# A mixture-of-experts stage: the side work of an expert unit gathered into one block, biases and embedding loaded a unit earlier

## The chip, the cores and the metric

The kernel runs on one core of a Trainium2 chip. The metric is device time in microseconds (us) of one execution. The engines are TensorE (PE, with its weight loads shown apart as PEld), VectorE (DVE), ScalarE (ACT), GpSimd (POOL) and SyncE (SP), whose queue issues most DMA transfers.

## The reference, cut to what matters

A first layer (attention beside a gated delta net) is followed by a second block on 256 tokens of width 1024: a mixer, a mixture of experts, a gate that adds a projected embedding, and a final norm. The change lies in the mixture of experts and in the place where the embedding is projected.

```python
def moe(u, w_router, b_router, w_gu, b_gu, w_dn, b_dn):      # 32 experts, top 4, 256 tokens
    ...
    def expert_block(args):
        e, xs = args
        hh = jnp.dot(xs, w_gu[e]) + b_gu[e]                  # 1024 -> 2048
        glu, lin = jnp.split(hh, 2, axis=-1)
        glu = jnp.minimum(glu, SWIGLU_LIMIT)
        lin = jnp.clip(lin, -SWIGLU_LIMIT, SWIGLU_LIMIT)
        act = glu * jax.nn.sigmoid(SWIGLU_ALPHA * glu) * (lin + 1.0)
        return jnp.dot(act, w_dn[e]) + b_dn[e]               # 1024 -> 1024
    ...
    yr = yb.reshape(n_rows, d) * row_gate[:, None].astype(yb.dtype)
    y = jax.ops.segment_sum(yr, row_tok, num_segments=t + 1)[:t]

# second_block, behind the mixer
    h = h + moe(rmsnorm_2(h, g_moe[i]), w_router[i], b_router[i], w_gu[i], b_gu[i], w_dn[i], b_dn[i])
    u = rmsnorm_2(h, g_ple[i])
    h = h + jax.nn.sigmoid(u @ w_ple_gate[i]) * (p[i] @ w_ple_proj[i])
```

## The kernel before

The mixture of experts takes about 1000 us of the time, from some 575 to 1572 us of the span. Each expert serves up to 64 tokens in a block. All 32 experts' weights are read: per expert 8 tiles of 1 MiB for the first product (`w_gu`, "gu" below) and 4 for the second (`w_dn`, "dn"), 384 transfers in all, issued by SP (L110) into 15 buffers in rotation, named raw, whi and wlo. `refill` issues the next transfer once a buffer is free and keeps 14 in hand, one fewer for each entry of `held`.

`run` (L1417) goes over 17 units. Unit 0 is one expert; units 1 to 7 and 9 to 16 are pairs, whose two experts' products use 64 columns each on the two halves of the TensorE array; unit 8 is one expert with two blocks of 64 tokens, which uses all 128 columns (L1445). In step i of the loop the gu products of unit i go into four PSUM tiles ph (L1455, 64 of them in a pair), the results are copied to hs (L1500, on DVE and ACT), and then the dn products of unit i - 1 go into two of the four PSUM tiles pm (L1455, 32 in a pair). `gated` (L1392, L1393) scales the result by the gates and `combine` puts the rows back to their tokens (PE L1401, DVE L1404).

Everything else of a unit is side work, written as generators that pause at each `yield`:

- `gather`: four comparisons on DVE (L1316) make the selection dd, 16 products of 128 columns (L1325) pick the tokens' rows, ACT copies them to xs (L1326). It runs for the unit after next.
- `activation`: 16 transposes of hs (L298; L1361 for the single unit), bias additions on DVE (L1372), clamps (L1376, L1378), Silu (ACT), and the product of both halves (L1381), in two halves z.
- `scatter_rows`: the comparisons dg (L1336), two transposes (L298), and their uses (L1343, L1344).
- `biases`: two transposes of the gates, then four products with the dn biases (L1551), once, in unit 3. `embed`: four transposes and eight products (L1623), once, near the end.

Before, a list `chores` holds these generators, and after every few products `chore()` runs one of them up to its next `yield`. The kernel is then built by a framework that keeps its own order of the instructions on each engine, so the order on an engine is not that of the code: rows of the order, where shown below, are the built kernel's. The place that the step of the loop takes for the products is this:

```python
                        for j in (0, 2):
                            products(kd, hp, k, x, ws, 0, 8, (j, j + 1))
                            if j:
                                refill()
                            chore()
```

Of the kernel before, what the change touches and what calls it, by code (L numbers as in the profile page):

```python
# [15 lines left out]
P = 128  # L16
# [50 lines left out]
def tile_net(ctx: ExitStack, tc: tile.TileContext, a: dict, dbg=None):  # L67
# [144 lines left out]
    def drain(g):  # L212
        for _ in g:
            pass
# [870 lines left out]
    with ExitStack() as c3:  # L1085
# [258 lines left out]
            V.tensor_reduce(b["gs"], ps.rearrange("p t k -> p (t k)"), AX.X, ALU.add)  # L1344
            yield

        def activation(b):

            kd = kind(b)
            n = 1 if kd == "single" else 2  # L1350
            m = 8 // n
            for z in range(n):
                gl = []
                for i in range(2):
                    ps = pm.tile([P, m, 64 * n], F32, name="pm")
                    for c_ in range(m):
                        q, k = (z * m + c_) // 2, c_ % 2
                        h = b["hs"][i][:, q * 2 * P + k:(q + 1) * 2 * P:2]
                        if n == 1:

                            T.matmul(ps[:, c_], h, cc("fold"), start=True, stop=True)  # L1361
                        else:
                            transpose(ps[:, c_], h)
                    gl.append(ps)
                for i in range(2):
                    ps = gl[i]
                    g = gl[i] = wk.tile([P, m, 64 * n], F32, name="sw", bufs=4)
                    cs = slice(i * 8 + z * m, i * 8 + z * m + m)
                    if kd == "pair":
                        bi = bguT[:, b["at"]:b["at"] + 2, cs].rearrange("p e c -> p c e")  # L1370
                        bi = bi[:, :, :, None].broadcast_to([P, m, 2, 64])
                        V.tensor_tensor(g.rearrange("p c (e s) -> p c e s", e=2), ps.rearrange("p c (e s) -> p c e s", e=2), bi, ALU.add)  # L1372
                    else:
                        V.tensor_tensor(g, ps, bc(b["places"][0]["bias"]()[:, cs], 64 * n), ALU.add)
                    if i:
                        V.tensor_scalar(g, g, 7.0, -7.0, ALU.min, ALU.max)  # L1376
                    else:
                        V.tensor_scalar(g, g, 7.0, None, ALU.min)  # L1378
                        A.activation(g, g, AF.Silu, scale=1.702)
                g, l = gl  # L1380
                V.scalar_tensor_tensor(g, l, 1.0, g, ALU.add, ALU.mult)  # L1381
                act = wk.tile([P, m, 64 * n], F32, name="act", bufs=4)
                A.activation(act, g, AF.Copy, scale=1 / 1.702)
                b["act"].append(act)
                yield
# [31 lines left out]
        def run(units, order, ready, more=None, room=None):  # L1417
# [36 lines left out]
                            first, last = c_ < 2, c_ >= nchunks - 2  # L1454
                        T.matmul(o[64 * i:64 * i + 64], x(i, c_), w_[:, zz, sl], start=first, stop=last)  # L1455

            chores = []

            def chore():
                while chores:  # L1460
                    try:
                        next(chores[0])
                        return
                    except StopIteration:
                        chores.pop(0)

            def flush():
                while chores:
                    chore()

            def after(i):
                chores.extend(f(held) for f in more.get(i, ()))

            for _ in gather(units[0]):
                pass
            after(-1)
            if n > 1:
                chores.append(gather(units[1]))
            done = []
            for i in range(n + 1):  # L1480
                if i < n:
                    b = units[i]
                    kd = kind(b)
                    xs = b["xs"]
                    x = lambda h, c_: xs[:, c_] if h is None else xs[:, c_, 64 * h:64 * h + 64] if kd == "pair" else xs[:, c_, :64]
                    hp = [ph.tile([P, 512], F32, name="ph") for _ in range(4)]
                    k = 0
                    while k < 8:
                        ws = [nxt() for _ in range(1 if kd == "double" else 2)]
                        for j in (0, 2):  # L1490
                            products(kd, hp, k, x, ws, 0, 8, (j, j + 1))
                            if j:
                                refill()
                            chore()
                        k += 2 if kd == "single" else 1
                    flush()
                    b["act"] = []
                    b["hs"] = [wk.tile([P, D], F32, name="hs", bufs=2) for _ in range(2)]
                    for j in (0, 2, 1, 3):
                        (V.tensor_copy if j // 2 else A.copy)(b["hs"][j // 2][:, j % 2 * 512:j % 2 * 512 + 512], hp[j])  # L1500
                    chores.append(activation(b))
                    if i == n - 1:
                        while len(b["act"]) < (1 if kd == "single" else 2):
                            chore()
                    chores.append(scatter_rows(b))
                if i:
                    b = units[i - 1]
                    kd = kind(b)
# [6 lines left out]
                    for q in range(4):  # L1515
                        ws = [nxt() for _ in b["places"]]
                        for z in range(0, 2, 2 if kd == "single" else 1):
                            products(kd, yp, 2 * q + z, x, ws, z, 8)
                            chore()
                        refill()  # L1520
                        if i == n:
                            chore()
                    while "gs" not in b:
                        chore()
                    gated(b, yp, room)
                    if i == n:
                        done.append(b)
                    else:
                        chores.append(combine(b))
                if i + 2 < n:  # L1530
                    chores.append(gather(units[i + 2]))
                after(i)
            flush()
            return done[0]

        def biases(held):

            gT = wk.tile([P, 2, P], F32, name="gT")
            bdn = [wk.tile([P, 512], F32, name="sw", bufs=4) for _ in range(2)]
            for nh in range(2):  # L1540
                nc.gpsimd.dma_start(bdn[nh][:NE], a["b_dn_2"][0][:, nh * 512:nh * 512 + 512])
            ps = pm.tile([P, 2, P], F32, name="pm")
            for t in range(2):
                transpose(ps[:NE, t], gate[:, t])
# [7 lines left out]
                    V.tensor_tensor(hres[:, t, ns], hres[:, t, ns], ps, ALU.add)  # L1552
                    yield

        nov = []

        def blocks(held):
            nov.append(nc.values_load(novi[0:1, 0:1], min_val=0, max_val=NJ))
# [40 lines left out]


        big = raw2, RAW2
        pv = []

        def embed(held):

            held.append(1)
            w_ = load(a["w_ple_proj_2"][0], 2, D)
            pt = wk.tile([P, 2, 256], F32, name="sw", bufs=4)
            nc.gpsimd.dma_start(pt, a["p_2"][0, 0].rearrange("(t p) d -> p t d", p=P))
            ps = pm.tile([P, 2, 2, P], F32, name="pm")  # L1610
            for t in range(2):
                for k in range(2):
# [13 lines left out]
            held.pop()  # L1626

        first = [lambda held, g=g: g() for g in (chosen, gates, changes, overflow)]
        last = run(units, order, ready, {-1: first, 2: [biases], 4: [blocks], len(units) - 3: [embed]})

        if "h3" in dbg:
            SY.dma_start(dbg["h3"].rearrange("(t p) d -> p t d", p=P), hres)
# [88 lines left out]
```

## Time and profile before

| | us |
|---|---|
| median of 3 runs | 1619.8 (1618.88 to 1620.29) |
| the profiled execution | 1618.85 |
| its span | 1617.1 |
| PE busy | 1550.6 (96%) |
| DVE busy | 630.6 (39%) |
| ACT busy | 420.5 (26%) |
| POOL busy | 27.9 (2%) |

The span is what the profiler sees between the first and the last instruction; the execution's own time is 1.75 us longer. Busy time of PE is counted from the start to the modelled end of its instructions, so that an engine that is busy all the time is not one at its peak. The trace has two records for each fp32 product: "x16" in a row of the trace are 8 products. The order counts products.

### The profile page before, as it was taken

The numbers are of one execution on the slowest core, as the hardware profiler recorded it, in microseconds if no ns is written. First come the engines' busy times: TensorE is split into PE (matmuls) and PEld (weight loads), VectorE is DVE, ScalarE is ACT, GpSimd is POOL, SyncE is SP. The second block draws the span as 40 slices with busy tenths as digits, with TensorE's granted clock in tenths as the row PEclk, the third lists the DMA queues.
The fourth block names the chain that finished last, engine by engine and source line by source line (L and its number), as shares of the span: only waits on it lengthen the run. The fifth ranks groups of instructions, "written<-read, shape, count | busy, mean of one in ns | idle before, by whom it ended". The sixth has DMA issues, their size and how long they took to land.

```text
span 1617.1 us, 20473 instructions
## 1 busy us (share of the span) xinstructions
PE 1550.6 (96%) x8162; PEld 955.7 (59%) x8162; DVE 630.6 (39%) x1183; ACT 420.5 (26%) x648; POOL 27.9 (2%) x39
## 2 busy tenths in 40 slices
PE   6999999999889989999999999999999999999996
PEld 6889899999688765444444444444444444444335
DVE  6867665456656651321321321331132132131136
ACT  4644554344457421110110110111011011011024
POOL 0000000000000000000000000000000000000001
PEclk9999999999899979999999999999999999999998
DMA  6443333345344199999999999999999999999981
GB/s 207 157 156 107 104 105 105 108 155 195 119 154 137 52 391 408 402 411 364 419 405 418 420 417 419 416 348 387 372 421 411 419 421 415 417 420 413 415 330 54
DMA packets 99247, 484.89 MB, mean 300 GB/s; under 512 B 10470, under 2 KB 14060, under 8 KB 49996
## 3 DMA queue, kind: packets, MB, share of 16 engines
q1 hardware_dynamic: 99004, 483.14, 75.8%
q8 instruction: 66, 1.08, 0.3%
q0 software_dynamic: 144, 0.39, 0.1%
q14 instruction: 33, 0.27, 0.0%
HBM read 482.46 MB, written 1.05 MB: 299 GB/s over the span
## 4 chain that ended last, share of the span: by engine, by line
PE 87%; DVE 7%; ACT 3%; issue 2%; POOL 1%; DMA 1%; SPq 0%; POOLq 0%; DVEq 0%; ACTq 0%
PE ph L1455 32%; PE pm L1455 14%; PE pm L298 5%; PE pm L1325 4%; PE pm L205 4%; PE pm L206 4%; PE pm L204 4%; DVE wlo L310 2%; PE pm L1401 2%; PE ph L1445 2%; PE pm L169 1%; PE pm L170 1%; PE pm L168 1%; ACT whi L309 1%; PE pm L626 1%
## 5 line engine op out<-in xcount | busy, mean ns | idle before, releaser
L1455 PE MATMUL ph<-raw,xs 128*64 128x512 f32 x928 | 266.4, 601 | 0.0
L1455 PE MATMUL ph<-whi,xs 128*64 128x512 f32 x528 | 198.5, 605 | 0.0
L1455 PE MATMUL ph<-wlo,xs 128*64 128x512 f32 x528 | 196.0, 599 | 0.0
L310 DVE TENSOR_TENSOR wlo<-raw,whi 128x2048 fp32r<-128x2048 f32 (+4 forms) x73 | 158.1, 2166 | 77.6 <-ACT whi L309 77.4
L204 PE MATMUL pm<-w,whi 128*128 128x256 f32 x640 | 183.1, 287 | 2.9 <-ACT w L309 2.0
L206 PE MATMUL pm<-w,wlo 128*128 128x256 f32 x640 | 179.3, 281 | 2.7 <-DVE wlo L310 2.7
L205 PE MATMUL pm<-w,whi 128*128 128x256 f32 x640 | 179.7, 281 | 1.9 <-DVE w L310 1.9
L1455 PEld LDWEIGHTS ph<-raw,xs 128*64 128x64 f32 x928 | 91.6, 137 | 139.6 <-issue 137.5
L309 ACT CAST whi<-raw 128x2048 fp32r<-128x2048 f32 (+4 forms) x73 | 131.9, 1808 | 153.7 <-PE pm L205 86.4
L1500 DVE COPY hs<-ph 128x512 f32<-128x512 f32 x34 | 23.5, 692 | 346.3 <-PE ph L1455 328.9
L1455 PE MATMUL pm<-raw,act 128*64 128x512 f32 x520 | 155.1, 598 | 0.0
L204 PEld LDWEIGHTS pm<-w,whi 128*128 128x128 f32 x640 | 122.2, 191 | 3.7 <-ACT w L309 2.5
L206 PEld LDWEIGHTS pm<-w,wlo 128*128 128x128 f32 x640 | 122.0, 191 | 3.1 <-DVE wlo L310 3.1
L205 PEld LDWEIGHTS pm<-w,whi 128*128 128x128 f32 x640 | 122.1, 191 | 2.7 <-DVE w L310 2.6
L1500 ACT COPY hs<-ph 128x512 f32<-128x512 f32 x34 | 18.4, 588 | 352.0 <-PE ph L1455 336.0
L1455 PEld LDWEIGHTS ph<-whi,xs 128*64 128x64 f32 x528 | 60.4, 138 | 80.0 <-issue 78.7
L1455 PEld LDWEIGHTS ph<-wlo,xs 128*64 128x64 f32 x528 | 59.4, 136 | 79.8 <-issue 79.0
L1455 PEld LDWEIGHTS pm<-raw,act 128*64 128x64 f32 x520 | 48.1, 136 | 71.7 <-issue 67.4
L1455 PE MATMUL pm<-wlo,act 128*64 128x512 f32 x232 | 90.2, 599 | 0.0
L1455 PE MATMUL pm<-whi,act 128*64 128x512 f32 x240 | 85.6, 598 | 0.0
L1326 ACT COPY xs<-pm 128x512 f32<-128x512 f32 (+1 forms) x34 | 19.5, 573 | 247.5 <-PE pm L1325 247.5
L1325 PEld LDWEIGHTS pm<-dd,w 128*128 128x128 f32 x544 | 66.8, 200 | 26.6 <-issue 25.7
(403 smaller groups left out, 2009.6 us busy)
## 6 DMA issues: line engine op xcount, KB each, us to landing
raw<-in_w_gu_dram SPq DMA_DIRECT2D x116, 1024.0 KB, 10.5
whi<-in_w_gu_dram SPq DMA_DIRECT2D x70, 1024.0 KB, 12.6
wlo<-in_w_gu_dram SPq DMA_DIRECT2D x70, 1024.0 KB, 10.7
raw<-in_w_dn_dram SPq DMA_DIRECT2D x65, 1024.0 KB, 7.6
raw<-in_w_in_dram SPq DMA_DIRECT2D x46, 1024.0 KB, 5.0
whi<-in_w_dn_dram SPq DMA_DIRECT2D x32, 1024.0 KB, 7.5
wlo<-in_w_dn_dram SPq DMA_DIRECT2D x31, 1024.0 KB, 7.6
raw<-in_w_branch_a_dram SPq DMA_DIRECT2D x4, 1024.0 KB
```

Of the source, the lines that this page charges most:

```text
L204: T.matmul(o, hi[:, k, ns], xh[:, k0 + k], start=first, stop=False)
L205: T.matmul(o, hi[:, k, ns], xl[:, k0 + k], start=False, stop=False)
L206: T.matmul(o, lo[:, k, ns], xh[:, k0 + k], start=False, stop=last)
L298: T.transpose(out, in_, ident[:k, :k])
L309: A.copy(hi, src)
L310: (by or V).tensor_tensor(lo, src, hi.bitcast(F32), ALU.subtract)
L1325: T.matmul(ps[:, c_, :n], ut[t][:, ds_], dd[:, t, :nb], start=t == 0, stop=t == 1)
L1326: A.copy(b["xs"][:, 4 * z:4 * z + 4, :n], ps[:, :, :n])
L1401: T.matmul(pss[nh], b["oh"][:, t], y[:, ns], start=i == 0, stop=i == 1)
L1445: T.matmul(o, x(None, chunk), ws[0][:, z, sl], start=chunk == 0, stop=chunk == nchunks - 1)
L1455: T.matmul(o[64 * i:64 * i + 64], x(i, c_), w_[:, zz, sl], start=first, stop=last)
L1500: (V.tensor_copy if j // 2 else A.copy)(b["hs"][j // 2][:, j % 2 * 512:j % 2 * 512 + 512], hp[j])
```

## The change

- The list `chores` and its steps between products go. All side work of a step of the loop is put into a list `todo` and run in one piece by `flush()`, behind the dn products.
- `activation` is split by its halves z into two generators, with `scatter_rows` between them.
- `gather` for the unit after next is started (its comparisons L1316) right behind the copies to hs, and so are the comparisons dg of `scatter_rows`; their products are run by `flush()`.
- `load_biases` loads the dn biases in step 2, `biases` uses them in step 3 (before, both in step 2's list). `load_embed` loads the embedding and its weight one step before `embed` uses them, and reserves a buffer (`held`) from then on. The small loads get tiles of their own, named bdn (before: two of the four tiles sw).
- The order of copies, sizes, engines and the arithmetic stay.

The diff, cut to its core:

```diff
-        def activation(b):
+        def activation(b, z):
...
-            for z in range(n):
+            if z < n:
...
-            chores = []
-
-            def chore():
-                while chores:
-                    try:
-                        next(chores[0])
-                        return
-                    except StopIteration:
-                        chores.pop(0)
+            todo = []
+
+            def start(g):
+
+                next(g, None)
+                todo.append(g)
 
             def flush():
-                while chores:
-                    chore()
+                for g in todo:
+                    drain(g)
+                todo.clear()
...
-                        for j in (0, 2):
-                            products(kd, hp, k, x, ws, 0, 8, (j, j + 1))
-                            if j:
-                                refill()
-                            chore()
+                        products(kd, hp, k, x, ws, 0, 8, range(4))
+                        refill()
                         k += 2 if kd == "single" else 1
-                    flush()
                     b["act"] = []
...
-                    chores.append(activation(b))
-                    if i == n - 1:
-                        while len(b["act"]) < (1 if kd == "single" else 2):
-                            chore()
-                    chores.append(scatter_rows(b))
+                    if i + 2 < n:
+                        start(gather(units[i + 2]))
+                    sc = scatter_rows(b)
+                    next(sc)
+                    todo += [activation(b, 0), sc, activation(b, 1)]
...
                             products(kd, yp, 2 * q + z, x, ws, z, 8)
-                            chore()
                         refill()
-                        if i == n:
-                            chore()
-                    while "gs" not in b:
-                        chore()
                     gated(b, yp, room)
                     if i == n:
                         done.append(b)
                     else:
-                        chores.append(combine(b))
-                if i + 2 < n:
-                    chores.append(gather(units[i + 2]))
+                        todo.append(combine(b))
+                flush()
                 after(i)
...
-        def biases(held):
-
-            gT = wk.tile([P, 2, P], F32, name="gT")
-            bdn = [wk.tile([P, 512], F32, name="sw", bufs=4) for _ in range(2)]
+        def load_biases(held):
+            bdn.extend(wk.tile([P, 512], F32, name="bdn", bufs=2) for _ in range(2))
             for nh in range(2):
                 nc.gpsimd.dma_start(bdn[nh][:NE], a["b_dn_2"][0][:, nh * 512:nh * 512 + 512])
+            yield
...
+        def load_embed(held):
+
+            held.append(1)
+            pt = wk.tile([P, 2, 256], F32, name="bdn", bufs=2)
+            nc.gpsimd.dma_start(pt, a["p_2"][0, 0].rearrange("(t p) d -> p t d", p=P))
+            emb.extend((load(a["w_ple_proj_2"][0], 2, D), pt))
+            yield
...
-        last = run(units, order, ready, {-1: first, 2: [biases], 4: [blocks], len(units) - 3: [embed]})
+        last = run(units, order, ready, {-1: first, 2: [load_biases], 3: [biases], 4: [blocks], len(units) - 4: [load_embed], len(units) - 3: [embed]})
```

What it does to the order on the engines is shown at three places. Names are tiles: ph and pm are the PSUM tiles of gu and of everything else, dd the selection of the gather, raw, whi and wlo weights, xs the gathered rows, act the activated ones, C the constants with the identity for transposes. The number behind x is a count of products.

PE, the gu products of a steady unit (unit 12), before:

```order
L1455 MATMUL ph<-raw,xs 64x512 x8
L1325 MATMUL pm<-dd,w_5715 128x128
L1325 MATMUL pm<-dd,w_5717 128x128
...
L1455 MATMUL ph<-raw,xs 64x512 x8
L1325 MATMUL pm<-dd,w_5717 128x128
L1325 MATMUL pm<-dd,w_5715 128x128
L1325 MATMUL pm<-dd,w_5717 128x128
L1455 MATMUL ph<-raw,xs 64x512 x8
L1455 MATMUL ph<-whi,xs 64x512 x8
L1455 MATMUL ph<-wlo,xs 64x512 x8
```

and the same unit in the changed kernel:

```order
L1455 MATMUL ph<-raw,xs 64x512 x24
L1455 MATMUL ph<-whi,xs 64x512 x8
L1455 MATMUL ph<-wlo,xs 64x512 x8
L1455 MATMUL ph<-whi,xs 64x512 x8
L1455 MATMUL ph<-wlo,xs 64x512 x8
L1455 MATMUL ph<-raw,xs 64x512 x8
L1455 MATMUL pm<-raw,act 64x512 x2
L1325 MATMUL pm<-dd,w_5715 128x128
```

The gather's products (13 and 3 of them) stood between gu products; they now stand behind the first two dn products, and the 64 gu products are one run.

PE, the dn products that follow in the same step, before:

```order
L1455 MATMUL pm<-raw,act 64x512 x2
L298 MATMUL pm<-C_66,hs 128x128 x9
L1455 MATMUL pm<-raw,act 64x512 x6
L298 MATMUL pm<-C_66,hs 128x128 x7
L298 MATMUL pm<-C_66,dg 128x128
L1455 MATMUL pm<-raw,act 64x512 x2
L298 MATMUL pm<-C_66,dg 128x128
L1455 MATMUL pm<-raw,act 64x512 x8
```

and in the changed kernel, from the first of the gather's last three products in the pass:

```order
L1325 MATMUL pm<-dd,w_5717 128x128
L298 MATMUL pm<-C_66,hs 128x128 x4
L1455 MATMUL pm<-raw,act 64x512 x6
L298 MATMUL pm<-C_66,hs 128x128 x4
L298 MATMUL pm<-C_66,dg 128x128 x2
L298 MATMUL pm<-C_66,hs 128x128
L1455 MATMUL pm<-raw,act 64x512 x2
L298 MATMUL pm<-C_66,hs 128x128 x7
L1455 MATMUL pm<-whi,act 64x512 x2
```

The runs of dn products were 2, 6, 2 and 22 long. They are now 2, 6 and 2, each followed by gather products (7, 6 and 3), then 6, 2 and 14 with the transposes between them.

PE, the embedding's products (L1623 before, L1619 in the changed kernel), before, with the dn products of unit 14 behind them:

```order
L1455 MATMUL ph<-wlo,xs 64x512 x4
L1623 MATMUL pm<-raw,sw 128x512 x8
L1455 MATMUL pm<-wlo,act 64x512
L1455 MATMUL pm<-raw,act 64x512
L1455 MATMUL pm<-wlo,act 64x512
L1455 MATMUL pm<-raw,act 64x512
L298 MATMUL pm<-C_66,hs 128x128 x8
```

and in the changed kernel:

```order
L298 MATMUL pm<-C_66,bdn 128x128 x4
L1619 MATMUL pm<-whi,sw 128x512
L1455 MATMUL pm<-raw,act 64x512 x6
L1619 MATMUL pm<-whi,sw 128x512
L1455 MATMUL pm<-raw,act 64x512 x2
L1619 MATMUL pm<-whi,sw 128x512 x2
L1455 MATMUL pm<-raw,act 64x512 x6
```

The eight products stood in one block between gu and dn products; they now stand one or two at a time between dn products of unit 14.

## Rows read from the trace of the kernel before

**Rows 1.** The page, busy time by engine, and shares of the chain by engine.
```profile
PE 1550.6 (96%) x8162; PEld 955.7 (59%) x8162; DVE 630.6 (39%) x1183; ACT 420.5 (26%) x648; POOL 27.9 (2%) x39
PE 87%; DVE 7%; ACT 3%; issue 2%; POOL 1%; DMA 1%; SPq 0%; POOLq 0%; DVEq 0%; ACTq 0%
```
**Rows 2.** Waits, SP's queue, 600:1560; us in total, times, longest us.
```profile
SPq L110 <- PE ph L1455: 465.2, 216, 12.1
SPq L110 <- PE pm L1455: 207.1, 98, 11.4
```
**Rows 3.** Windows: us, engines' busy time (instructions), PEclk, DMA share, GB/s.
```profile
1180.00:1480.00 300.00, 295.14 (x1242) 126.74 (x1242) 64.00 (x136) 30.68 (x50) 0.74 (x1) 1.00 1.01 418
1240.00:1260.00 20.00, 19.01 (x74) 7.46 (x74) 7.94 (x18) 3.89 (x6) 0.00 (x0) 1.00 1.01 420
```
**Rows 4.** Timeline, PE, gu: start, us, instruction, records, idle before and releaser.
```profile
1201.07 0.64 PE L1455 MATMUL ph<-whi,xs 128*64 128x512 f32 x1
...
1261.26 5.42 PE L1455 MATMUL ph<-raw,xs 128*64 128x512 f32 x16
1266.62 3.17 PE L1325 MATMUL pm<-dd,w 128*128 128x128 f32 x26
1269.71 5.42 PE L1455 MATMUL ph<-raw,xs 128*64 128x512 f32 x16
1275.07 0.94 PE L1325 MATMUL pm<-dd,w 128*128 128x128 f32 x6
1275.93 0.64 PE L1455 MATMUL ph<-raw,xs 128*64 128x512 f32 x1
...
1299.07 1.23 PE L298 MATMUL pm<-C,hs 128*128 128x128 f32 x8
```
**Rows 5.** Timeline, PE, the dn products of a steady unit.
```profile
1238.88 1.23 PE L298 MATMUL pm<-C,hs 128*128 128x128 f32 x8
...
1240.79 0.64 PE L1455 MATMUL pm<-wlo,act 128*64 128x512 f32 x1
...
1242.56 1.88 PE L1455 MATMUL pm<-wlo,act 128*64 128x512 f32 x4
1244.37 1.10 PE L298 MATMUL pm<-C,hs 128*128 128x128 f32 x7
1245.78 0.33 PE L298 MATMUL pm<-C,dg 128*128 128x128 f32 x1 [0.31 <-DVE sw L1372]
1246.04 1.93 PE L1455 MATMUL pm<-wlo,act 128*64 128x512 f32 x4
1247.90 0.33 PE L298 MATMUL pm<-C,dg 128*128 128x128 f32 x1
1248.16 0.64 PE L1455 MATMUL pm<-whi,act 128*64 128x512 f32 x1
...
1258.65 0.50 PE L1401 MATMUL pm<-yh,ohT 128*128 128x512 f32 x1
```
**Rows 6.** Timeline, PE: where a run of 48 gu products begins, and its successor.
```profile
1100.80 0.64 PE L1455 MATMUL ph<-whi,xs 128*64 128x512 f32 x1
...
1123.88 0.70 PE L1445 MATMUL pm<-wlo,act 128*128 128x512 f32 x1
```
**Rows 7.** Timeline, PE: dn products beside the double unit.
```profile
1066.41 1.94 PE L1455 MATMUL pm<-raw,act 128*64 128x512 f32 x8
1068.28 1.22 PE L298 MATMUL pm<-C,hs 128*128 128x128 f32 x8
```
**Rows 8.** The unit with the biases: timeline of PE, and two windows.
```profile
744.53 6.23 PE L1455 MATMUL ph<-whi,xs 128*64 128x512 f32 x16
750.69 1.98 PE L1551 MATMUL pm<-sw,gT 32*128 32x512 f32 x4
743.00:746.00 3.00, 3.00 (x8) 0.99 (x8) 1.37 (x2) 0.00 (x0) 0.00 (x0) 0.86 1.03 429
746.00:749.00 3.00, 3.00 (x10) 1.02 (x8) 0.00 (x0) 0.00 (x0) 0.00 (x0) 0.57 0.65 268
```
**Rows 9.** The page: GB/s moved, in 40 slices of the span.
```profile
GB/s 207 157 156 107 104 105 105 108 155 195 119 154 137 52 391 408 402 411 364 419 405 418 420 417 419 416 348 387 372 421 411 419 421 415 417 420 413 415 330 54
```

More of the change, by code (lines that the diff above doesn't have):

```diff
@@ L1455, in products @@
                         T.matmul(o[64 * i:64 * i + 64], x(i, c_), w_[:, zz, sl], start=first, stop=last)
-            chores = []
-            def chore():
-                while chores:
-                    try:
-                        next(chores[0])
-                        return
-                    except StopIteration:
-                        chores.pop(0)
+            todo = []
+            def start(g):
+                next(g, None)
+                todo.append(g)
             def flush():
-                while chores:
-                    chore()
+                for g in todo:
+                    drain(g)
+                todo.clear()
             def after(i):
-                chores.extend(f(held) for f in more.get(i, ()))
-            for _ in gather(units[0]):
-                pass
+                todo.extend(f(held) for f in more.get(i, ()))
+            drain(gather(units[0]))
             after(-1)
             if n > 1:
-                chores.append(gather(units[1]))
+                start(gather(units[1]))
+            flush()
             done = []
@@ L1528, in run @@
                     else:
[L1529 to L1531 removed]
+                        todo.append(combine(b))
+                flush()
                 after(i)
@@ L1534, in run @@
             return done[0]
+        def load_biases(held):
+            bdn.extend(wk.tile([P, 512], F32, name="bdn", bufs=2) for _ in range(2))
+            for nh in range(2):
+                nc.gpsimd.dma_start(bdn[nh][:NE], a["b_dn_2"][0][:, nh * 512:nh * 512 + 512])
+            yield
         def biases(held):
             gT = wk.tile([P, 2, P], F32, name="gT")
-            bdn = [wk.tile([P, 512], F32, name="sw", bufs=4) for _ in range(2)]
-            for nh in range(2):
-                nc.gpsimd.dma_start(bdn[nh][:NE], a["b_dn_2"][0][:, nh * 512:nh * 512 + 512])
             ps = pm.tile([P, 2, P], F32, name="pm")
@@ L1553, in biases @@
                     yield
-        nov = []
+        bdn, nov = [], []
         def blocks(held):
@@ L1601, in tile_net @@
         big = raw2, RAW2
-        pv = []
+        pv, emb = [], []
+        def load_embed(held):
[4 more added lines that the diff above has]
+            yield
         def embed(held):
[L1606 to L1609, printed above, removed]
+            w_, pt = emb
             ps = pm.tile([P, 2, 2, P], F32, name="pm")
```

## The prediction

> **What bounds the kernel now.** The page comes first: TensorE (PE) is busy for 96% of the span, and 87% of the chain that ended last lies on it [rows 1]. Next come the waits of the SP queue, which issues the weights: it waits 465.2 and 207.1 us for products to free a weight buffer [rows 2], so PE holds the transfers up and not they PE. The windows then show how near the second limit is: over 300 us of steady units the granted clock is 1.00, PE works 295.14 us of them, and the transfers run all the time too, at 418 GB/s; 20 us of it have 420 [rows 3]. At 420 GB/s one tile of 1 MiB (1,048,576 bytes) takes 2.497 us, and the 24 tiles of a pair unit 59.92 us. The unit lasts 1261.26 - 1201.07 = 60.19 us [rows 4]. So PE sets the pace, with the transfers 0.27 us behind it.
>
> **What a broken run of products costs.** In the timeline each fp32 product is two records. The two experts of a pair sit on the two halves of the array, and while both halves are fed a pair of products takes 0.886 us: the run of 48 lasts 1123.88 - 1100.80 = 23.08 [rows 6], the run of 8 lasts 5.36 (1261.26 to 1266.62) [rows 4], and 17.72 us for the 20 further pairs is 0.886. A run of 8 should then take 3.54, and takes **1.82 more**. For dn products the run of 22 takes 10.49 (1248.16 to 1258.65) and the run of 6 takes 3.58 (1240.79 to 1244.37) [rows 5]: 0.864 a pair, and **1.0 a run** on top, as the run of 2 confirms (1246.04 to 1247.90, 1.86). The reason is in the order: four gu products of one expert come before four of the other, so at each end of a run one half stands alone. The row at 1242.56 shows such an end: four records of one tile in 1.88 us, without a partner [rows 5]. Where a and b alternate from the first product, the extra is gone: 4 products took 1.87 (1066.41 to 1068.28) [rows 7], 0.14 above two pairs. Long runs are worth something only by the number of such ends that they save.
>
> **The change, part by part.** The order shows that the block is not undivided. In a steady unit all 64 gu products now stand in one run that the first two dn products close, but the side work is spread between dn products: 64+2, 6, 2, 6, 2, 14 against 8, 8, 48+2, 6, 2, 22. Six runs each.
>
> *A steady unit.* Products before: 5.36 + 5.36 + 23.14 (1275.93 to 1299.07) [rows 4] + 3.58 + 1.86 + 10.49 = 49.79. After: 64+2 is 23.14 + 8 x 0.886 = 30.23; 3.58, 1.86, 3.58, 1.86; and 14 is 10.49 - 4 x 0.864 = 7.03. Sum 48.14, so -1.65. Side work before: gather products 3.09 + 0.86 [rows 4]; transposes 1.91 (1238.88 to 1240.79), 1.41 + 0.26 (1244.37 to 1246.04) and 0.26 [rows 5], 7.8 in all. Of these some 0.7 are waits for a PSUM bank that the bias additions (L1372) free; the 0.31 at 1245.78 is one. After: the 26 records of 3.09 and the 6 of 0.86 give 0.223 a product and 0.2 a block, so 7, 6 and 3 of them take 1.76, 1.54 and 0.87; the same 18 transposes some 2.5; one bank wait of 0.63 remains (an estimate: seven transposes stand behind one run of 2, 1.86 us, and two additions of some 0.65). That is 7.35, so -0.45. The combine stays 2.61. Together **60.2 to 58.1**, -2.1.
>
> *The whole stage, by counting ends in the two orders.* (a) Twelve pair units (2 to 7, 9, 11 to 15) lose two gu runs of 8: 24 x 1.82 = **-43.7**. (b) Eleven dn passes (of units 1 to 6 and 9 to 13) get two more short runs: 22 x 1.0 = **+22.0**. (c) The dn pass of unit 7, beside the double unit, had four alternating runs (0.14 each) and gets six of the other kind: **+5.4**. (d) The dn pass of unit 14 takes the embedding's eight products, before one block between runs, now one or two at a time between dn products. Before: a gu end of 1.8 and four alternating runs, 2.4; after: eight ends, 8.0; and since a buffer is reserved one unit longer here I add 1.5 for one late tile: **+7.2**. (e) The biases add two short runs and save an end of about 1: **+1.2**. (f) Unit 10 loses five short gu runs (three alternating, two of one pair, 2.4) and is cut twice by combines: **-2**. (g) The start, where a single gu product now stands between two gathers: **+1**. Products: **-8.9**.
>
> Side work: nine steady units at -0.45 are -4.0. Against it, behind the dn pass of the double unit 16 gather products and 18 transposes now stand in one stretch with no product to cover the bias additions, and the first embedding product follows its own transposes at once; two or three bank waits and copies of 0.4 to 1 us each, together +3. Net **-1**.
>
> The clock: the bias unit of before has the only low stretch in the stage. Its product run took 6.16 where the like took 5.36 (744.53 to 750.69), and the granted clock was 0.86 and 0.57 in the 3 us windows there [rows 8]: 3 x 0.14 + 3 x 0.43 = 1.7 us of PE. The four bias products are now spread between dn products. I count half: **-0.9**; bounds -1.7 and 0.
>
> Sum -10.8. The profiled execution took 1618.85, 1 us under the median of 1619.8: 1608.05, so **1608.0**.
>
> *Edits at no cost.* The gather's compares (L1316) are started behind the copies of ph. Their products stand right behind the gu run, but DVE's order has each set of compares a whole unit ahead (it waits only until PE has used the last set), so PE does not meet them. What waits behind them on DVE is the first bias addition, whose bank PE needs 3.58 us later; four compares are under 1 us. If that cover went, it would be at most 0.74 a unit, 10 us in all; I take nothing. The loads of biases and embedding move one unit ahead: two small ones on POOL's queue, which issues nothing else in the stage that PE waits for, and one tile of 1 MiB on SP's, past 24 weight tiles. It takes its 2.5 us of transfer either way, and a slot of 15 for a unit longer, which is in (d). What the early loads save is no more than the wait for the first of them, and I see none on PE of before at the embedding; taken at nothing.
>
> **Rivals.**
>
> *The transfers become the bound.* A unit of 58.1 asks for 24 tiles in less than their 59.92. Each steady unit then eats 1.8 us of the lead; five or six stand before the double unit, five behind it. For it: 1.01 of DMA share already [rows 3]. Against it: SP's longest waits for PE are 12.1 and 11.4 us with a tile landing in some 10 [rows 2], so the lead is several units deep, and the stage has transfer time to spare, since the page's slices at 348, 387 and 372 GB/s show 72, 33 and 48 GB/s below 420 over 40 us each, some 15 us of full rate [rows 9]. If the lead is used up from the start, steady units gain 0.27 and the dear places (c) to (e) stay hidden behind the transfers: -0.27 x 14 = -4, **1615**. Chance 0.11.
>
> *The clock falls in the broken dn pass.* Slower than before: a pass now has five stretches of transposes and gather products between runs as short as one pair. If each of the 14 drops as the bias unit did, 1.7 us each, that is +24 on the forecast: **1632**. It is slower than before from the seventh drop and by over 0.2% from the ninth. For it: the one drop followed small products between runs [rows 8]. Against it: the steady units of before have stretches of 9 and 7 transposes around a run of 6 and hold 1.00 through 300 us [rows 3, 5]. Chance 0.07.
>
> *Ends cost nothing of their own.* The row says that a run of 8 takes 5.36 and not 3.54 [rows 4]. [...] Were it the latter, side work and clock alone would remain: -1.9, **1617**. Chance 0.05.
>
> *The change does not do what it says.* It does not quite: the order splits the block. The forecast is made for the order as built.
>
> **How the numbers follow.** Forecast 0.77. Its own range: the bank waits (0 to 6), the late tile (0 to 3), the clock (-1.7 to 0) and 0.1 on each of the 22 ends that are added give about 1603 to 1612. To leave out no more than 2 in 10 it reaches to the transfers' case: **1603 to 1615.5**. A measurement of this kernel tells 0.2%, 3.2 us, from no change. Faster: 0.77 and half of the transfers' case, 0.82. Same: the other half and the third rival, 0.11. Slower: 0.07.
>
> **What would show it.** A steady unit of 58.1 between combines; one gu run of 30.2; runs of 6 and 2 at 3.6 and 1.9; SP still waiting for PE. Wrong would be: PE waiting for tiles in units 5 to 7 or 13 to 15 (first rival), clock under 1.00 in the dn passes (second), runs of 2 at 0.9 (third), or a dn pass of unit 14, with the embedding in it, much beyond 34 us.

## The result, and the profile after

| | kernel before | changed kernel |
|---|---|---|
| median, us | 1619.34 (1617.16 to 1620.29, 4 runs) | 1610.28 (1607.14 to 1613.31, 4 runs) |
| ratio, 95% interval | | 0.9946 [0.9924, 0.9968] |
| profiled execution, us | 1618.85 | 1613.31 |
| span, us | 1617.1 | 1611.4 |

The changed kernel is faster by 0.54%, 9 us; the forecast was 1608.0 in a range from 1603 to 1615.5. The page of the changed kernel, against [rows 1], has 6 us less of PE in the same count of records:

```profile
PE 1544.6 (96%) x8162; PEld 959.1 (60%) x8162; DVE 627.6 (39%) x1183; ACT 420.0 (26%) x648; POOL 27.9 (2%) x39
```

The timeline of PE shows where. These are the rows of one steady unit, to be held against [rows 4, 5] (start, us, instruction, records, idle before):

```profile
1201.11 0.64 PE L1455 MATMUL ph<-whi,xs 128*64 128x512 f32 x1
...
1231.34 1.83 PE L1325 MATMUL pm<-dd,w 128*128 128x128 f32 x14
...
1236.68 1.60 PE L1325 MATMUL pm<-dd,w 128*128 128x128 f32 x12
1238.21 1.93 PE L1455 MATMUL pm<-wlo,act 128*64 128x512 f32 x4
1240.07 0.94 PE L1325 MATMUL pm<-dd,w 128*128 128x128 f32 x6
1240.85 0.64 PE L298 MATMUL pm<-C,hs 128*128 128x128 f32 x4
...
1244.99 0.74 PE L298 MATMUL pm<-C,hs 128*128 128x128 f32 x4
1245.57 0.38 PE L298 MATMUL pm<-C,dg 128*128 128x128 f32 x2
1246.52 0.39 PE L298 MATMUL pm<-C,hs 128*128 128x128 f32 x1 [0.56 <-DVE sw L1372]
1246.84 1.93 PE L1455 MATMUL pm<-whi,act 128*64 128x512 f32 x4
1248.70 1.11 PE L298 MATMUL pm<-C,hs 128*128 128x128 f32 x7
1249.74 0.64 PE L1455 MATMUL pm<-wlo,act 128*64 128x512 f32 x1
...
1256.80 0.50 PE L1401 MATMUL pm<-yh,ohT 128*128 128x512 f32 x1
```

The run of 64 gu and 2 dn products lasts 1231.34 - 1201.11 = 30.23 us (forecast 30.23). The gather's three pieces take 1.76, 1.53 and 0.78, and one wait of 0.56 for a bias addition stands at 1246.52. The side work comes to 7.5 us where 7.35 was forecast, and the unit to 58.30 instead of 58.1. Four units in a row (from 1201.1 to 1434.3) have it.

The windows (us, busy time of PE, PEld, DVE, ACT and POOL, clock, DMA share, GB/s) and the waits of SP's queue (us in total, times, longest) show what that asks of the transfers, against [rows 2, 3]:

```profile
590.00:605.00 15.00, 13.46 (x54) 11.65 (x55) 8.70 (x56) 0.74 (x2) 1.18 (x2) 0.50 1.02 409
1200.00:1260.00 60.00, 59.15 (x257) 25.95 (x257) 14.51 (x32) 6.14 (x10) 0.00 (x0) 1.00 1.01 421
```
```profile
SPq L110 <- PE ph L1455: 301.0, 180, 17.1
SPq L110 <- PE pm L1455: 198.6, 80, 8.8
SPq L110 <- DMA raw<-in_w_dn_dram: 59.5, 34, 4.6
...
SPq L110 <- PE pm L1619: 20.1, 1, 20.1
```

SP waits less for PE (500 us where it was 672) and more behind other transfers. The lead of a tile is the time from its landing to its first use. It is worked out here for the first two tiles of each dn pass, from the ends of the DMA packets and the starts of the products; where PE waits for tiles, as in most units of e3 below, the same working gives 0 to -2 us, so it is good to some 2 us. In the kernel before the lead is some 18 us in every steady unit (17.7 to 18.0 in units 4 to 6 and 11 to 13). In the changed kernel it falls by some 1.65 us a unit: 11.3 us in unit 1 and 8.0 in unit 3, 12.7 in unit 4 (behind the longer unit with the biases) and 9.4 in unit 6; behind the double unit, which takes 12 tiles in some 50 us, 14.9 in unit 9 and 8.4 in unit 13. Then it is 4.1 and 2.2 us, and the last two tiles of the stage land about 1 us before their use. So at the end there was next to nothing left, but PE did not run out of tiles. No wait of PE from 600 to 1560 us names one (of its weight loads' waits 2 us in all do); a late tile need not show as a wait, since in e9 below these waits are 7.5 us in all and every unit is some 4 us longer, but the runs keep their price too: the last 32 dn products take 14.3 us (1551.89 to 1566.22), and 16 pairs at 0.864 are 13.8.

Seen from the first gather to the first product of the last combine the stage is 11.3 us shorter in the profiled executions (588.62 to 1574.90 before, 593.85 to 1568.83 after). The changed kernel's profiled execution came to the stage 5.2 us later and is the slowest of its four; the code ahead of the stage is the same in both kernels, and e1, e2, e5, e7 and e9 below, which share it, came there at 587.9 to 590.4. So the spans of the two profiled executions differ by only 5.7 us. Why the medians differ by 9.1 and not by 11.3 no run shows.

### The profile page after: what moved, and what is told of

It is laid out like the page before. It is cut to its first block, busy times and chain, and to the rows that moved or that the text cites. A ratio compares the mean times of both kernels' runs of the same rounds, so it can differ in the third digit from the quotient of the medians.

```text
span 1611.4 us, 20470 instructions
## 1 busy us (share of the span) xinstructions
PE 1544.6 (96%) x8162; PEld 959.1 (60%) x8162; DVE 627.6 (39%) x1183; ACT 420.0 (26%) x648; POOL 27.9 (2%) x39
## 5 line engine op out<-in xcount | busy, mean ns | idle before, releaser
L1455 PE MATMUL ph<-raw,xs 128*64 128x512 f32 x928 | 245.1, 599 | 0.0
L1455 PE MATMUL ph<-wlo,xs 128*64 128x512 f32 x536 | 189.8, 599 | 0.0
L1455 PE MATMUL ph<-whi,xs 128*64 128x512 f32 x520 | 185.1, 598 | 0.0
L1455 PE MATMUL pm<-raw,act 128*64 128x512 f32 x528 | 176.0, 601 | 0.0
L1455 PEld LDWEIGHTS ph<-raw,xs 128*64 128x64 f32 x928 | 88.0, 137 | 126.6 <-issue 126.1
L1455 PEld LDWEIGHTS pm<-raw,act 128*64 128x64 f32 x528 | 51.7, 136 | 81.8 <-issue 76.9
L1455 PE MATMUL pm<-whi,act 128*64 128x512 f32 x240 | 92.1, 601 | 0.0
L1325 PE MATMUL pm<-dd,w 128*128 128x128 f32 (+1 forms) x544 | 77.0, 296 | 1.1 <-issue 1.1
## 6 DMA issues: line engine op xcount, KB each, us to landing
raw<-in_w_dn_dram SPq DMA_DIRECT2D x66, 1024.0 KB, 14.4
```

Source lines behind the costliest of these rows:

```text
L1325: T.matmul(ps[:, c_, :n], ut[t][:, ds_], dd[:, t, :nb], start=t == 0, stop=t == 1)
```

## The experiments

**The block alone, and the loads alone.** The first kernel is the changed one with the loads left in the generators that use them (the embedding is then used one unit later):

```diff
-        last = run(units, order, ready, {-1: first, 2: [load_biases], 3: [biases], 4: [blocks], len(units) - 4: [load_embed], len(units) - 3: [embed]})
+        last = run(units, order, ready, {-1: first, 2: [biases], 4: [blocks], len(units) - 3: [embed]})
```

> The changed kernel with the loads of biases and embedding left where they were (the embedding is therefore used one unit later). Theory (the gain is the exchange of dear ends of gu runs for cheaper ends of dn runs): steady unit 58.3 us as in the changed kernel, total within 3 us of the changed kernel, 1607 to 1613. Rival (the early loads carry a part of the gain): at least 4 us slower than the changed kernel, 1614 or more.

Measured: 1607.38 us, ratio 0.9926 [0.9911, 0.9940], steady unit 58.3. The block carries the whole gain; the early loads give nothing that can be told. The second kernel is the reverse, the kernel before with load_biases and load_embed:

> The kernel before with only the loads of biases and embedding one unit earlier. Theory: steady unit unchanged at 60.2 us, total within 2 us of the kernel before, 1617 to 1621. Rival (the loads carry a part of the gain): 1615 or less.

Measured: 1640.35 us, ratio 1.0129 [1.0114, 1.0145]. Neither theory had this: alone, the early loads cost 21 us. SP's timeline, two windows and two rows of PE's timeline of this kernel:

```profile
1400.99 0.39 SPq L110 DMA_DIRECT2D wlo<-in_w_ple_proj_dram  x1
...
1434.23 41.39 SPq L110 DMA_DIRECT2D wlo<-in_w_gu_dram  x2
```
```profile
1440.00:1460.00 20.00, 19.22 (x81) 9.20 (x82) 3.15 (x5) 1.17 (x2) 0.00 (x0) 1.00 0.21 88
1460.00:1480.00 20.00, 20.00 (x63) 7.21 (x60) 0.00 (x0) 2.34 (x4) 0.00 (x0) 1.00 0.17 65
```
```profile
1458.08 5.42 PE L1455 MATMUL ph<-raw,xs 128*64 128x512 f32 x16
1463.43 2.84 PE L1631 MATMUL pm<-wlo,sw 128*128 128x512 f32 x6
```

The embedding's weight takes a buffer of the rotation at 1401 and gives it back after its last product at 1475. Fifteen transfers later the rotation comes to that buffer, and the queue stands 41 us: the two issues from 1434.23 on last to 1475.62, and the next one stands at 1475.84. The lead falls from 17.8 us (unit 13) to nothing (unit 14), and PE waits in the units behind: the next 64 gu products take 37.2 us (1517.56 to 1554.73), where 32 x 0.886 + 1.82 = 30.2 is their price. Not all of the 21 us is the queue's. The scheduler's order changed too: the embedding's products now cut the gu run, so that unit 15 has four runs of 8 where it had two, and the dn pass behind has the runs of a steady unit (16.8 us) where it had four alternating ones (14.4). That is some 6 us, an estimate (2 x 1.82 + 2.4); no run parts the two. The changed kernel has the stop of the queue in small: one wait of 20.1 us for a product of L1619, above. There the lead paid for it, down to its last microseconds.

**The order of the code, kept on PE.** In two kernels each PE instruction of the stage is tied behind the one before it in the code, so that the scheduler cannot move it:

```diff
+            m = nc.tensor.matmul(*args, **kw)
+            return tc.keep_in_program_order(m) if pinned else m
```

From the kernel before, this makes pieces of 4, 8, 4, 44+4, 4, 8 and 16+4 products with side work between them, as the code has it, and the two experts' products alternate. In the rows all products then have the lines of the wrapper, L74 and L78.

> The kernel before with TensorE kept in the order of the code in the expert stage: side work still between gu products, but the products of the two experts alternate from the first of a run to the last. Theory (an end costs 1.0 to 1.8 us because four products of one expert stand before four of the other): a run of 8 gu products takes 3.6 to 3.8 us instead of 5.36, and a run of 4 takes 1.9; TensorE needs some 54 us for a steady unit, less than the 59.9 of its 24 transfers, so the steady unit settles at 59.9 us with TensorE waiting for tiles, and the total falls by 5 to 20 us, to 1600 to 1614. Rival (ends cost nothing by themselves, the place of the side work decides): run of 8 still over 5 us, total as before within 3 us or slower. Rival (many short pieces let the clock fall): granted clock under 1.00 in the steady units and slower than 1625.

Measured: 1596.28 us, ratio 0.9855 [0.9841, 0.9868], 23 us and so more than the 5 to 20 expected. The timeline of PE:

```profile
666.18 3.65 PE L74 MATMUL ph<-raw,xs 128*64 128x512 f32 x16
669.76 2.05 PE L74 MATMUL pm<-dd,w 128*128 128x128 f32 x16
671.74 1.94 PE L74 MATMUL ph<-raw,xs 128*64 128x512 f32 x8
...
700.52 3.65 PE L74 MATMUL pm<-raw,act 128*64 128x512 f32 x16
704.10 0.44 PE L78 MATMUL pm<-C,dg 128*128 128x128 f32 x2
```

The same 8 products take 3.58 us (666.18 to 669.76) that took 5.36 [rows 4], and a unit that still has a lead takes 51.2 us. Later units take 60.4, near the 59.9 that 24 tiles take to land. Side work between gu products thus costs next to nothing by itself (a run of 4 takes 1.87, 0.1 above two pairs); what the order of the two experts costs, e10 below shows. The waits of this kernel now name tiles, among them one that was not expected, 27.6 us for the embedding's weight, which is requested where it is used and whose product PE may not pass any more:

```profile
PE pm L74 <- DMA raw<-in_w_ple_proj_dram: 27.6, 1, 27.6
PE ph L74 <- DMA raw<-in_w_gu_dram: 12.3, 10, 1.3
```

Around that wait the granted clock falls too, to 0.84 in 1380 to 1440 us and 0.93 in 1440 to 1500, where every window from 660 us to there has 1.00.

From the changed kernel the same edit makes what the change says in words, 64 gu products, 32 dn products and all side work in one piece:

> The changed kernel with TensorE kept in the order of the code in the expert stage: 64 gu products, 32 dn products, then the side work in one piece, which is what the change says in words; the two experts' products alternate. Theory: one run of 64 and 32 products takes 42.3 us, side work and combine 10 plus 2 to 4 of waits for the bias additions, 55 us in all, less than the 59.9 of the transfers; a steady unit starts under 57 us and settles at 59.9 once the lead of 20 us is used up; total at the transfers' limit, 1595 to 1608. Rival (the block without product cover costs more than the ends give): steady unit over 60 us from the first, total 1615 or more.

Measured: 1594.61 us, ratio 0.9856 [0.9839, 0.9873]. The first units take 51.0 us, later ones 60.4. In a window of 60 us PE works only 52 us, at 421 GB/s:

```profile
1260.00:1320.00 60.00, 51.69 (x250) 20.96 (x250) 12.12 (x29) 6.24 (x10) 0.00 (x0) 1.00 1.01 421
```

So the two places for the side work come out alike once the experts alternate (also in e8 and e11 below, where the embedding disturbs neither), and both end near the transfers.

**Which order is dear.** e3 with two products of one expert ahead of two of the other in every group of four:

```diff
+                    for i in range(2):
+                        for j in js:
+                            T.matmul(outs[j][64 * i:64 * i + 64], x(i, chunk), ws[i][:, z, j * 512:j * 512 + 512], start=chunk == 0, stop=chunk == nchunks - 1)
```

> The kernel of e3_pin_before with one thing altered: within each group of four products (two of each expert) both of the first expert come first; every block stays where it is. Theory (the order of the two experts makes the end dear): a run of 8 gu products takes 4.4 to 4.5 us instead of 3.58, a run of 4 takes 2.7 instead of 1.87; the units before the lead is used up take 57 us instead of 51; the total, which the transfers bind, moves by less than 4 us from e3_pin_before (1592 to 1600). Rival (the run of 5.36 in the kernel before had another cause): run of 8 unchanged at 3.6.

Measured: 1598.85 us, ratio 0.9873 [0.9858, 0.9888]; the total is as expected and the run is not. 8 products take 3.64 us (672.95 to 676.59), and 4 take 1.87, nothing more than when they alternate:

```profile
672.95 3.70 PE L74 MATMUL ph<-raw,xs 128*64 128x512 f32 x16
676.59 2.05 PE L74 MATMUL pm<-dd,w 128*128 128x128 f32 x16
```

The theory fell in its simple form. The next kernel has four ahead of four in gu, as in the kernel before, in a fixed order (side work stands behind every eight products):

> The kernel of e3_pin_before with the four gu products of the first expert before the four of the second, as in the kernel before; side work stands behind every eight gu products instead of every four. Theory, mended after e6_skew (a half of the array is served past at most two waiting products of the other, so that two in a row cost nothing and four in a row set the second expert back by two products): a run of 8 gu products takes 5.3 to 5.4 us, against 3.6 in e3 and e6; units before the lead is used up take 55 to 59 us instead of 51; total at the transfers' limit or a little above it, 1594 to 1606. Rival (the 5.36 came from the scheduler's places and not from the order of the experts): run of 8 at 3.6 us.

Measured: 1622.56 us, ratio 1.0016 [1.0007, 1.0025].

```profile
685.03 5.42 PE L74 MATMUL ph<-raw,xs 128*64 128x512 f32 x16
690.38 2.05 PE L74 MATMUL pm<-dd,w 128*128 128x128 f32 x16
```

The 5.35 us are back (685.03 to 690.38), and a unit takes 58.4, 7.2 more than in e3, which is four gu ends of 1.8. So the run and the unit came as the mended theory had them. The total did not, and missed the expected 1594 to 1606 by 17 us. The kernel gains 1.8 us on the 60.2 of each steady unit, but the step with the embedding takes 82.6, 24 more than its neighbours, where the kernel before has 66.6. The 24 are a wait for the embedding's weight, the eight products themselves (9.2, where the kernel before has 7.06 for them) and two more gu ends (3.6):

```profile
PE pm L74 <- DMA raw<-in_w_ple_proj_dram: 10.9, 1, 10.9
```

e3 has this wait too (27.6 us), but there the transfers, which bind, go on under it (a DMA share of 0.99 in 1380 to 1440 us) and most of it is paid back: e11 below, without it, is 5.7 us faster.

**What the lead is made of.** First with fewer tiles requested ahead:

```diff
-                while len(ready) < slots() - 1 - len(held):
+                while len(ready) < slots() - 1 - 8 - len(held):
```

> The changed kernel with eight weight tiles fewer requested ahead (6 instead of 14), nothing else. Eight tiles are 20.0 us of transfer. In the changed kernel the lead of a tile's landing over its use falls by 1.65 us a steady unit, from 20.2 us in the first dn pass to 11.3, and after the double unit from 24 to 9.6. Theory (the gain is lent by the lead, since a steady unit of 58.3 us asks for more than the transfers' 59.9 give): with 20 us less, TensorE waits for tiles in nearly all steady units, they settle at 59.9, and the total is 1622 to 1632, the gain gone. Rival (the transfers have room of their own): TensorE still does not wait, 1608 to 1614.

Measured: 1612.83 us, ratio 0.9967 [0.9954, 0.9980]. This did not touch what it was meant to: the lead is 17.0 us at the first dn pass and 11.2 at the second, as in the changed kernel (17.1 and 11.3). The reading of it, argued and not shown, is that the number in hand sets where a request stands in the code, and that SP issues it when its buffer is free in any case. So the buffers themselves were taken away, 7 in rotation instead of 15:

```diff
-    raws += [(raw2, "raw", RAW2), (raw2, "whi", 2), (raw2, "wlo", 2), (st, "whi", HL), (st, "wlo", HL)]
+    raws += [(raw2, "raw", RAW2)]
...
-            ready = ahead(order, RAW + RAW2 + 4)
+            ready = ahead(order, RAW + RAW2 - 1)
```

> The changed kernel with 7 weight buffers in rotation instead of 15, nothing else. In e5_hand8 the lead was still 20 us, as with 14 tiles in hand, so the number in hand does not set it; the buffers do. Eight buffers are 20.0 us of transfer. Theory (the gain of 1.9 us a steady unit is lent by the lead): TensorE waits for tiles in nearly all steady units, they settle at 59.9 us, and the total is 1620 to 1634, the gain gone. Rival (the transfers have room of their own): steady units stay at 58.3 and the total within 4 us of the changed kernel.

Measured: 1678.92 us, ratio 1.0363 [1.0347, 1.0379]. The gain is gone, as the theory had it, and 59 us more with it, far beyond the expected 1620 to 1634. At the first dn tiles no lead is left (0 to -2 us), and units take 62 to 64, more than 59.9, since with so few buffers the transfers pause as well: a run of 64 products wants 16 tiles in 30 us, and in the dn pass behind it all buffers are full for a while. The second row is such a stretch:

```profile
1320.00:1330.00 10.00, 10.00 (x34) 3.60 (x31) 1.38 (x2) 1.17 (x2) 0.00 (x0) 1.00 1.02 423
1280.00:1290.00 10.00, 9.43 (x43) 4.12 (x42) 5.83 (x14) 1.89 (x3) 0.00 (x0) 1.00 0.87 340
```

The kernel before was not run with 7 buffers. So e9 shows that the changed kernel needs the buffers, and not how much of this loss belongs to the change.

**The embedding in the common row of transfers.** Its weight is made one more tile of the order, requested and used in turn, with no buffer reserved:

```diff
+            if len(units) > 1 and i == len(units) - 2:
+                yield a["w_ple_proj_2"][0], 2, D, "(k p) n -> p k n"
...
-            w_, pt = emb
+            w_, pt = take[0](), emb[0]
```

In the changed kernel:

> The changed kernel with the embedding's weight taken as one more tile of the common row of transfers, requested and used in its turn, so that no buffer is reserved for it and the queue of transfers is not held up behind it; the scheduler then also puts the eight embedding products in one block behind the dn products of unit 14. Theory: the dn pass of unit 14 loses the short runs (eight ends of 1.0 become two), and the 22.9 us that the queue stood still there go; 5 to 8 us faster than the changed kernel, 1602 to 1606. Rival (both are hidden): within 2 us of the changed kernel.

Measured: 1602.53 us, ratio 0.9896 [0.9881, 0.9911]. The two timelines of unit 14's dn pass, the changed kernel first, then this one:

```profile
1464.45 0.66 PE L298 MATMUL pm<-C,bdn 128*128 128x128 f32 x4
1465.90 1.12 PE L1619 MATMUL pm<-whi,sw 128*128 128x512 f32 x2 [0.78 <-DVE sw L1611]
1466.95 3.65 PE L1455 MATMUL pm<-raw,act 128*64 128x512 f32 x12
1470.53 1.13 PE L1619 MATMUL pm<-whi,sw 128*128 128x512 f32 x2
1471.59 1.93 PE L1455 MATMUL pm<-raw,act 128*64 128x512 f32 x4
```
```profile
1461.25 0.66 PE L298 MATMUL pm<-C,bdn 128*128 128x128 f32 x4
...
1463.60 12.18 PE L1459 MATMUL pm<-raw,act 128*64 128x512 f32 x52
1475.71 7.13 PE L1622 MATMUL pm<-whi,sw 128*128 128x512 f32 x16
```

The dn products run through and the eight embedding products follow in one block. From the first product of one combine to that of the next the step takes 56.3 us (1428.39 to 1484.73) instead of 65.0 (1431.72 to 1496.71). In e4 the same edit, and in e3 its like:

> e4_pin_after with the embedding's weight as one more tile of the common row of transfers. e4 is bound by the transfers from its third unit on, and they stand at 0.87 of their time in 1440 to 1500 us, where the queue waits for the buffer of the embedding's weight. Theory: that is 8 us of transfer time lost, and they come back: 1585 to 1590. Rival (the end is set by TensorE there): within 2 us of e4, 1593 to 1597.

Measured: 1590.02 us, ratio 0.9823 [0.9810, 0.9836]: 4.6 us of the 8 came back, just at the upper edge of the theory's 1585 to 1590.

> e3_pin_before with the embedding's weight as one more tile of the common row of transfers. In e3 TensorE waits 27.6 us for that tile, which is requested only when it is used, and the transfers stand at 0.81 of their time in 1440 to 1500 us. Theory: both go, and since the transfers bind the rest, what comes back is the transfer time lost, some 12 us: 1581 to 1588. Rival (the lead that piles up in that wait pays for the units behind it): within 4 us of e3, 1592 to 1600.

Measured: 1590.54 us, ratio 0.9817 [0.9804, 0.9831]: between the theory and its rival. The wait is gone, 5.7 us of 12 came back. In the stretch that stood at 0.81 in e3 the transfers are now busy, but the stretch before it has 0.88. These two are the fastest kernels of the study, 1.8% under the kernel before.

```profile
1380.00:1440.00 60.00, 55.78 (x238) 20.74 (x236) 11.00 (x22) 7.41 (x12) 0.74 (x1) 1.00 0.88 361
1440.00:1500.00 60.00, 51.07 (x228) 18.02 (x226) 12.41 (x24) 5.07 (x8) 0.00 (x0) 1.00 1.01 421
```

## Why the prediction was right, point by point

**The bound.** PE set the pace before, and it still does after, to the last pass: the runs keep their price, and SP still waits 500 us for PE.

**The price of an end of a gu run (1.82).** Right, and shown: the same 8 products take 3.58 when the experts alternate (e3) and 5.35 when four stand ahead of four (e10).

**The price of a dn run (1.0).** The size was right and the reason only in part. The prediction saw that one half stands alone at the end of a run, and blamed the order of the experts there too; in e6 two ahead of two cost nothing (3.64 us for 8 products, against 3.58 in e3). What the rows have is a count. The run of 2 is two products of one expert ([rows 5], four records of wlo), the run of 6 holds two of that expert and four of the other, and that of 22 ten and twelve. Their times go with the fuller half, at 0.864 a product and 0.13 on top, which is read off the run of 2: 2 x 0.864 + 0.13 = 1.86 (measured 1.86), 4 x 0.864 + 0.13 = 3.59 (3.58), 12 x 0.864 + 0.13 = 10.50 (10.49), and for the new run of 14 (six and eight) 8 x 0.864 + 0.13 = 7.04, measured 7.06 (1249.74 to 1256.80). Three of the four rows are those from which the price was taken, so only the last one tests it here. e3 is a second test: with both halves even, 8 dn products take 3.58 (700.52 to 704.10), no more than the uneven run of 6. The sum came out right because the scheduler cuts the new runs at the same uneven places.

**The steady unit.** Forecast 58.1, measured 58.30, that is -1.9 where -2.1 was forecast. The products came within 0.03 (48.17 for 48.14). The side work gave -0.27 instead of -0.45: the 18 transposes took 2.9 where 2.5 was counted, and the gather's pieces and the bank wait gave 0.2 of that back.

**The sum.** The stage, from the first gather to the last combine, can be cut at the combines of units 3, 9 and 13 and held against the terms (the +3 of side work halved between its two places):

| stretch of the stage, us | forecast | measured |
|---|---|---|
| to the combine of unit 3: start, biases | -4.5 | -2.2 |
| to that of unit 9: the double unit | -3.0 | -3.0 |
| to that of unit 13: four steady units | -8.4 | -7.5 |
| to the last: the embedding | +5.1 | +1.4 |
| sum | -10.8 | -11.3 |

The middle came as counted. The start and the steady units gave 3.2 less than forecast, and the end cost 3.7 less, so that the sum is this close in part by luck. The embedding's spreading is dear all the same: e7, which takes it and the held buffer away, is 8.7 us faster in that step. Of the 1.5 for a late tile in (d) nothing was seen on PE; the queue did stand 20.1 us there. Which of the other terms of the end was too high stays open.

**The clock.** Of the 1.7 us in the bias unit half was counted. The bias products of the changed kernel run from 823.9 to 832.8 us, and the clock stays at 1.00 there, so all of it came:

```profile
820.00:840.00 20.00, 19.28 (x68) 6.78 (x64) 4.45 (x7) 1.07 (x2) 0.74 (x1) 1.00 1.01 417
```

On the other side stands the start. Two gathers now run in a stretch with a granted clock of 0.50 (590 to 605 us, above), and the second takes 5.51 us to the next product where it took 3.77, as the changed kernel's row and the one of before show:

```profile
602.75 5.59 PE L1325 MATMUL pm<-dd,w 128*128 128x128 f32 x32
```
```profile
610.86 3.84 PE L1325 MATMUL pm<-dd,w 128*128 128x128 f32 x32
```

The clock is at 0.50 for 20.5 us there where it was for 17.1 (worked out from the clock of windows of 1 us), and the two gathers with the first 32 gu products take 28.3 us to the next product (593.85 to 622.14) where they took 26.0 (588.62 to 614.63). Against these 2.3 us the prediction had +1, for (g). What set the clock there was not tried.

**The rivals.** The transfers' case was right in its mechanism: the lead is eaten at 1.65 us a unit (1.8 was said). The prediction called the lead several units deep; it is 18 us in the kernel before, under a third of a unit, and lasts because a unit takes so little of it and because the biases' and the double unit refill it. It reached the last tiles with about 1 us to spare, a margin that the prediction had not worked out, so that this rival stayed away narrowly. The clock did not fall in the dn passes (1.00 in all windows from 660 to 1560 us). That ends cost nothing, a run of 8 at 3.54 us and 1617 in all, is refuted by e10 beside e3: with four ahead of four the run takes 5.35, and 3.58 when the experts alternate. That the change does not do what it says held: done as it says (e4), it gains 25 us and not 9.

**The loads at no cost.** Right within the measurement for the changed kernel, but by a margin that the prediction did not see: the buffer given back late stops the queue, and only the lead hides it. In the kernel before the same edit costs 21 us (e2), some 6 of them by the order. The prediction sized this risk by one late tile, 1.5 us.

## What to carry to other kernels

Where two halves of the array are fed in turn, count for each run of products how many each half gets and in which order, before counting the pieces into which side work cuts it: alternating pieces of four cost 0.1 us each here, and four ahead of four cost 1.8 us at each end. The 1.9 us that PE gained in each steady unit here were lent by the lead of the transfers, at 1.65 us a unit; ask how much lead there is and where it is refilled. And a tile that stayed in the rotation of buffers stopped the queue when the rotation came round, for 20.1 us in the changed kernel and 41 us in e2, far from the place where it was loaded.

## What the runs showed of the hardware that was not expected

Products of one half of the array were started ahead of earlier ones of the other half. In the kernel before the order has four products of raw ahead of four of whi (the last chunk of unit 11's gu run); the trace starts the first of whi at 1235.25, while the last records of raw start up to 1236.53. In e10, where the code fixes this order, it is the same (whi from 697.68, raw up to 698.96).

```profile
1235.25 0.64 PE L1455 MATMUL ph<-whi,xs 128*64 128x512 f32 x1
1235.67 0.59 PE L1455 MATMUL ph<-raw,xs 128*64 128x512 f32 x1
1235.73 0.59 PE L1455 MATMUL ph<-whi,xs 128*64 128x512 f32 x1
...
1236.53 0.59 PE L1455 MATMUL ph<-raw,xs 128*64 128x512 f32 x1
```

The first product of whi thus stands 1.28 us before the last record of raw, in both kernels, and so ahead of about two products of raw (the last four records, at 0.43 us each). With two ahead of two 8 products take 3.64 us (e6), as good as the 3.58 when the experts alternate (e3); with four ahead of four they take 5.35 (e10), and the 1.77 more are two pairs of 0.886. What sets this, in the engine or in its queue, was not shown: no order but these was run.
